# Two ready times in the plan of TensorE's work: the first tokens' key and query rows, and the sample's attention weights

## The chip, the cores and the metric

The kernel runs on one core of one Trainium2 chip. The metric is device time in microseconds (us) of one execution. The kernel before takes 1882.4 us, the median of three timed runs (1882.38 to 1887.38).

## What is computed

One step of a hybrid encoder layer, for a prompt of 2048 new tokens and a sample of 64 further tokens of a stream with 4096 past ones. The width is 1024, all data is float32. Shortened:

```python
h = rmsnorm(x, norm_g) @ w_in                      # 1024 -> 6144 columns
qa, ka, va, za, qb, kb, vb, zb, ga, gb = split(h)
qa, ka = rmsnorm(qa, qn_g), rmsnorm(ka, kn_g)      # per head and half, 64 wide
# branch A, 4 heads: two softmaxes of 64-wide halves, ALiBi, block-causal in chunks of 64
s = einsum(qa, ka) * 64 ** -0.5 - slope * |q_pos - k_pos|
p = softmax(where(allowed, s, -inf))
oa = (p[:, 0] - lam * p[:, 1]) @ va
# branch B, 4 heads: retention in chunks, with a state per head
ob = (qb @ kb.T * decay) @ vb + xi * qb @ state
oa = rmsnorm(oa, subln_g) * 0.2 * silu(za)
ob = rmsnorm(ob) * silu(zb)
y = x + (sigmoid(ga) * (oa @ w_oa) + sigmoid(gb) * (ob @ w_ob)) @ w_out
```

The prompt's tokens attend to each other, the sample's 64 tokens to the cache of 4096 keys and values and to themselves. Keys, values and retention states are outputs too.

## The kernel before

Every float32 matmul of the projections is done as three: each operand is split into a high part (a cast to fp32r, names ending in h or "hi") and a low part (the rest, l or "lo"), and high x high, high x low and low x high are added up in PSUM. ScalarE makes the high parts, VectorE or GpSimd the low ones.

**Stages.** The prompt goes through the input projection in two halves of 1024 tokens. In the first half the value, key and query columns come first, 512 columns at a time over tiles of 128 tokens (L1137 in `mm_group`). Each tile is finished by a routine of its own: `fin_va` for values, `fin_qk` for keys and queries. The other columns of the first half are done by Strassen's scheme (L989 in `strassen`). Beside these runs the sample's attention: per head nine score blocks (`sample_attn`, L2055 to L2057), their softmax, and in `sample_pv` the product with the values (L2258). When the last head is done, the x of the second half is scaled (`x_scaled`, L514 on TensorE and L528 on VectorE) and split (`x_split`, L561 and L563), to stand ready when the first half ends. The second half's projection (L1137, 256 or 288 tokens at a time for the transposed columns) then runs between blocks of the prompt's attention (scores L1880 and L1881, transposed weights L1992, product with the values L1970 to L1972) and of retention (L2337 to L2410). The last columns (L1566) and the output stage (from L2673) follow.

**Who sets the order.** Nothing is ordered by hand; the lists of TensorE, ScalarE and VectorE stand in the order in which the program was built. The kernel builds it with a planner of its own: each routine is a Python generator that issues instructions and yields the time at which it can go on. The class keeps a clock for each engine (`self.pe`, `self.act`, `self.dve`, `self.pool`, `self.dma`) and moves it by a fixed cost for each instruction. `loop` always resumes the routine of best priority whose time has come on TensorE's clock. So a number that a routine yields is not a wait on the chip: it decides behind how many other instructions the routine's next ones are put in the list. On the chip semaphores make an instruction wait for its data, and what stands behind it in the engine's list waits with it.

```python
LAT = 250.0
SLACK = 400.0
LAND = 2000.0
def P(self, cycles):
    self.pe += cycles / 2.4 + 13.0
    return self.pe + LAT
def V(self, n, ready=0.0, rate=1.05):
    self.dve = max(self.dve, ready) + rate * n + 155
    return self.dve + LAT
```

Numbers are nanoseconds of the plan. Buffers are planned in the same way: `take` waits for one, `give` states when it is free again. Buffers that the steps touch: "ev" (3), "thi" (1) and "tlo" (2) in `fin_qk`; "ath" (2), "atl" (2) and "V" (2 in the first half) in the sample's attention; the PSUM banks "mm", "s" and "at" (2 each), "pv" and "tp" (1 each).

**The two places.** In `fin_qk` the rows of a tile are multiplied by their inverse roots (L1325, VectorE, into `raw`); then four transposes (L1340) put them into bank "tp", ScalarE and VectorE take high and low parts (L1355 and L1356 for keys, L1350 and L1351 for queries), and SP's queue stores them. `t0` is the tile's first token: it is 0 for the first tile of the first half only, once for keys and once for queries. In `sample_pv` the weights of a head are transposed in five groups (L2273, into bank "at"); for each of two parts ScalarE casts (L2287), VectorE subtracts (L2289), and `mms` multiplies them with the split values (L2258). The part's ready time is what `parts` holds; `mms` yields it ahead of its matmuls. The weights themselves come from L2241, which needs rows that were swapped between partitions by way of memory (row<-swap).

## Time and profile before

| what | value |
|---|---|
| median of the timed runs | 1882.4 us |
| the profiled execution's own time | 1886.05 us |
| its span, first to last instruction | 1883.4 us |
| TensorE busy (PE) | 1866.8 us, 11090 matmuls |
| weight loads (PEld) | 1644.6 us |
| VectorE (DVE), ScalarE (ACT), GpSimd (POOL) | 1328.1, 975.3, 678.6 us |
| granted TensorE clock | 1.000 on average |

How to read it: PE is TensorE's matmuls, PEld its weight loads, which run beside them; SPq is the queue from which the DMAs are issued. A row of a timeline has the start, the duration, the engine, the line, the operation, what is written and read, and how many like ones follow each other; in brackets stands how long the engine was idle before it, and what ended that. Matmul records overlap: the time that one takes from the list is the distance from its start to the next one's. A row of waits has the total, the number of times and the longest. A row of a stage table has the stretch and its length, then the busy time of PE, PEld, DVE, ACT and POOL with the numbers of instructions, the granted clock, the DMA share and GB/s. A row for one line of the kernel has minimum, median and maximum duration in nanoseconds and the first and last start.

### The profile page before, as it was taken

To read this page: it belongs to the slowest core of one execution; us is meant where nothing else is said; L and a number is where in the kernel's file an instruction comes from. 1 tells how busy PE (TensorE), PEld (TensorE's weight loads), DVE (VectorE), ACT (ScalarE), POOL (GpSimd) and SP (SyncE) were. 2 spreads that over 40 slices of the span, in tenths; PEclk is the share of its full clock that TensorE was granted. 3 is DMA by queue.
4 is the path that set the end of the run, shared out by engine and by line. 5 is a ranking of instruction groups with operands and counts; after the bars stand their busy time and mean duration, and the time that the engine had idled before them with its cause. 6 is when DMAs were issued, how large, how long until landed. Compare 5 with 4: busy or idle time off the path is not lost.

```text
span 1883.4 us, 33013 instructions
## 1 busy us (share of the span) xinstructions
PE 1866.8 (99%) x11090; PEld 1644.6 (87%) x11090; DVE 1328.1 (71%) x3112; ACT 975.3 (52%) x2266; POOL 678.6 (36%) x728
## 2 busy tenths in 40 slices
PE   9999999999999999999999999999999999999999
PEld 7788878888888789888988889899999999998887
DVE  6765856658585678787587877777876769887664
ACT  6444545554434566555455655556666446654221
POOL 2420366555552122122210344253224555532442
PEclk9999999999999999999999999999999999999999
DMA  7654555666767967565523659446437988886552
GB/s 255 216 175 123 161 166 169 176 200 198 240 189 186 253 198 190 152 174 169 145 72 101 172 136 238 129 123 154 126 109 234 259 250 255 263 257 211 165 157 78
DMA packets 402555, 340.07 MB, mean 181 GB/s; under 512 B 85329, under 2 KB 348625, under 8 KB 401362
## 3 DMA queue, kind: packets, MB, share of 16 engines
q1 hardware_dynamic: 402386, 337.97, 61.8%
q8 instruction: 87, 1.43, 0.3%
q14 instruction: 82, 0.67, 0.1%
HBM read 218.27 MB, written 118.75 MB: 179 GB/s over the span
## 4 chain that ended last, share of the span: by engine, by line
PE 82%; DMA 7%; DVE 5%; ACT 2%; SPq 2%; issue 1%; POOL 1%; DVEq 0%; ACTq 0%; POOLq 0%
PE mm L1137 27%; PE mm L989 8%; PE tp L989 4%; PE at L1992 3%; PE s L1880 2%; PE s L1881 2%; PE s L989 2%; PE pv L1972 2%; PE pv L1971 2%; PE pv L1970 2%; DMA ws<-in_w_in_dram 2%; PE s L2799 1%; PE s L2798 1%; PE s L2797 1%; SPq L280 1%
## 5 line engine op out<-in xcount | busy, mean ns | idle before, releaser
L748 POOL TENSOR_TENSOR wl<-ws,wh 128x512 fp32r<-128x512 f32 x107 | 148.9, 1402 | 256.4 <-ACT wh L727 181.5
L1137 PE MATMUL mm<-wh,xh 128*128 128x512 f32 x504 | 203.0, 403 | 0.0
L1137 PE MATMUL mm<-wh,xl 128*128 128x512 f32 x504 | 198.2, 393 | 0.0
L1137 PE MATMUL mm<-wl,xh 128*128 128x512 f32 x504 | 198.0, 393 | 0.1
L1137 PE MATMUL mm<-xh,wh 128*128 128x288 f32 (+2 forms) x544 | 179.8, 330 | 0.0
L1137 PE MATMUL mm<-xh,wl 128*128 128x288 f32 (+2 forms) x544 | 175.6, 323 | 0.0
L1137 PE MATMUL mm<-xl,wh 128*128 128x288 f32 (+2 forms) x544 | 175.5, 323 | 0.0
L1920 ACT ACTIVATE row<-row,a_mx 128x1024 f32<-128x1024 f32 (+7 forms) x144 | 149.8, 1042 | 11.9 <-DVE a_mx L1899 11.9
L2008 DVE TENSOR_TENSOR atl<-at,ath 128x512 fp32r<-128x512 f32 (+1 forms) x144 | 92.6, 658 | 76.6 <-ACT ath L2006 76.3
L2006 ACT CAST ath<-at 128x512 fp32r<-128x512 f32 (+1 forms) x144 | 79.1, 564 | 106.6 <-PE at L1992 106.0
L856 POOL TENSOR_TENSOR wl<-ws,wh 128x256 fp32r<-128x256 f32 x64 | 54.8, 856 | 199.0 <-ACT wh L847 198.9
L1747 POOL TENSOR_TENSOR r_y<-r_y,r_sq 128x256 f32<-128x256 f32 x32 | 28.3, 884 | 238.2 <-DVE r_sq L1744 154.5
L1137 PEld LDWEIGHTS mm<-wh,xl 128*128 128x128 f32 x504 | 94.6, 188 | 21.5
L1137 PEld LDWEIGHTS mm<-wl,xh 128*128 128x128 f32 x504 | 95.0, 188 | 18.5 <-POOL wl L748 0.9
L1137 PEld LDWEIGHTS mm<-wh,xh 128*128 128x128 f32 x504 | 94.8, 188 | 17.8 <-DVE raw L1308 0.2
L1137 PEld LDWEIGHTS mm<-xh,wh 128*128 128x128 f32 x544 | 102.4, 188 | 7.2
L1137 PEld LDWEIGHTS mm<-xl,wh 128*128 128x128 f32 x544 | 102.5, 188 | 6.9
L1137 PEld LDWEIGHTS mm<-xh,wl 128*128 128x128 f32 x544 | 102.3, 188 | 6.6
L1889 DVE CUSTOM_DVE_ANT_0 row<-s,dfar 128x512 f32<-128x512 f32 (+2 forms) x141 | 87.1, 629 | 23.8 <-PE s L1881 18.0
L1942 DVE SCALAR_TENSOR_TENSOR row<-row,a_w 128x1024 f32<-128x1024 f32 (+5 forms) x88 | 96.9, 1106 | 0.0
L1880 PE MATMUL s<-K,q 128*128 128x512 f32 (+3 forms) x240 | 90.5, 378 | 1.2 <-DVE a_acc L1889 1.2
L727 ACT CAST wh<-ws 128x512 fp32r<-128x512 f32 x111 | 67.7, 620 | 41.4 <-DMA ws<-in_w_in_dram 12.7
(543 smaller groups left out, 6075.4 us busy)
## 6 DMA issues: line engine op xcount, KB each, us to landing
ws<-in_w_in_dram SPq DMA_DIRECT2D x155, 256.0 KB, 3.5
q<-qT SPq DMA_DIRECT2D x128, 128.0 KB, 3.9
K<-kT SPq DMA_DIRECT2D x48, 256.0 KB, 4.7
V<-vN SPq DMA_DIRECT2D x24, 512.0 KB, 5.9
row<-in_x_prompt_dram SPq DMA_DIRECT2D x16, 512.0 KB, 4.6
wz<-in_w_in_dram SPq DMA_DIRECT2D x32, 256.0 KB, 4.3
row<-in_cache_k_T_dram SPq DMA_DIRECT2D x32, 256.0 KB, 3.2
row<-in_cache_v_diff_dram SPq DMA_DIRECT2D x32, 256.0 KB, 3.8
```

The costliest lines, as they stand in the source:

```text
L727: self.nc.scalar.copy(h, st)
L748: eng.tensor_sub(l, st, h.bitcast(F32))
L856: nc.gpsimd.tensor_sub(l[:, cs], src, h[:, cs].bitcast(F32))
L989: nc.tensor.matmul(ps, w[:, c], xs[x][c], start=bool(tag) and c == 0 and i == 0, stop=c == 3 and i == 2, skip_group_check=True)
L1137: nc.tensor.matmul(ps, p, q, start=c == 0 and i == 0, stop=c == KC - 1 and i == 2)
L1880: nc.tensor.matmul(ps, q1s, kk, start=True, stop=False)
L1889: nc.vector.tensor_tensor_reduce(out=row[:, k0:k0 + n], in0=ps, in1=tab, scale=-SLOPES[h], scalar=3.0e38, op0=ALU.add, op1=ALU.min, accum_ ...
L1920: nc.scalar.activation(u, u, AF.Exp, bias=mx, scale=-1.0, accum_out=lp[:, k:k + 1])
L1942: nc.vector.scalar_tensor_tensor(out=u0, in0=u1, scalar=w[:, 0:1], in1=u0, op0=ALU.mult, op1=ALU.add)
L1992: nc.tensor.transpose(at[:, w:w + 128], src, self.ident)
L2006: nc.scalar.copy(ah[:, :w], at[:, :w])
L2008: nc.vector.tensor_sub(al[:, :w], at[:, :w], ah[:, :w].bitcast(F32))
```

## The change

Two ready times are raised. In `fin_qk` the first tile's transposes may come 2000 ns after the plan's end of the row, where it was 400 (for keys and for queries, tokens 0 to 127 only). In `sample_pv` every part of the weights counts as ready 2000 ns after its low part, where it was 500.

```diff
@@ fin_qk @@
             nc.vector.tensor_mul(raw3, raw3, rs.unsqueeze(2).to_broadcast([r, ng, 64]))
-            t = self.V(n + 100) + SLACK
+            t = self.V(n + 100) + (LAND if t0 == 0 else SLACK)
             yield t
@@ sample_pv @@
                 nc.vector.tensor_sub(s[:, :, 1], c, s[:, :, 0].bitcast(F32))
                 t2 = self.V(64 * nt, t2)
-                parts.append((a, tag, t2 + 500))
+                parts.append((a, tag, t2 + LAND))
             self.give("at", t2)
```

Each engine has the same number of instructions as before (10790 on TensorE, 3114 on VectorE, 2039 on ScalarE, 733 on GpSimd, 1544 DMAs on SP); a few are put into another bank. But since every later decision of the planner hangs on its clocks, the order of the lists is another one from the first edited place on: on TensorE from the 372nd instruction to the 7767th, behind which its list is the same row for row but for the names of buffers.

On TensorE at the first key tile (mm is the projection of a later tile, raw the normalised key rows of the first), this piece of the difference:

```order
 L1137 MATMUL mm<-wl,xh_120 128x512
 L1137 MATMUL mm<-wh,xl_121 128x512
+L1137 MATMUL mm<-wh,xh_120 128x512
+L1137 MATMUL mm<-wl,xh_120 128x512
+L1137 MATMUL mm<-wh,xl_121 128x512
+L1137 MATMUL mm<-wh,xh_120 128x512
+L1137 MATMUL mm<-wl,xh_120 128x512
+L1137 MATMUL mm<-wh,xl_121 128x512
 L1340 MATMUL tp<-ident,raw 128x128 x4
 L1137 MATMUL mm<-wh,xh_120 128x512
```

Six matmuls of the projection have moved ahead of the four transposes; the transposes stand at place 378 in place of 372.

On TensorE at the first head's product with the values (at is the bank of the transposed weights, atp a split part of them, vhl the split values; L989 is Strassen's scheme), before:

```order
L2273 MATMUL at<-ident,row 128x128 x8
L989 MATMUL mm<-S1h,wh 128x512
L989 MATMUL mm<-S1l,wh 128x512
L989 MATMUL mm<-S1h,wl 128x512
L989 MATMUL mm<-S1h,wh 128x512
L989 MATMUL mm<-S1l,wh 128x512
L989 MATMUL mm<-S1h,wl 128x512
L989 MATMUL mm<-S1h,wh 128x512
L989 MATMUL mm<-S1l,wh 128x512
L989 MATMUL mm<-S1h,wl 128x512
L2258 MATMUL pv<-vhl,atp 128x256 x8
```

The same eight matmuls in the order of the change, with the eleven rows that end in the next transposes:

```order
L989 MATMUL tp<-xh_122,wh 128x512
L989 MATMUL tp<-xl_123,wh 128x512
L989 MATMUL tp<-xh_122,wl 128x512
L2055 MATMUL s<-ath,qq 128x512
L2056 MATMUL s<-atl,qq 128x512
L2057 MATMUL s<-ath,qq 128x512
L989 MATMUL tp<-xh_122,wh 128x512
L989 MATMUL tp<-xl_123,wh 128x512
L989 MATMUL tp<-xh_122,wl 128x512
L2258 MATMUL pv<-vhl,atp 128x256 x8
L2273 MATMUL at<-ident,row 128x128 x4
```

The eight rows of transposes that stood together are now two groups of four (places 1282 and 1301), and a score block of the next head and more of Strassen's scheme stand ahead of the matmuls, which move from place 1260 to 1320. Over the four heads the lag grows: the last L2258 stands at 2486 in place of 2402, the first L514 of the second half's x at 2509 in place of 2425, and the first half's last L989 at 2665 in both. The first score of the prompt's attention (L1880) stands at 2858 in place of 2801.

On TensorE in the second half, where retention blocks run between projection and attention (row is their working memory, tp and pv the banks that they choose from; L2410 transposes one block's result, L2371 and L2374 make the next block's), before, with buffer numbers:

```order
L2410 MATMUL tp_7565<-ident_106,row_6182 128x128 x4
L1880 MATMUL s_7571<-K_6616,q_7099 128x512
L1881 MATMUL s_7571<-K_6616,q_7099 128x512
L1137 MATMUL mm_7487<-xh0_120,wh_7401 128x512
L1137 MATMUL mm_7487<-xl0_121,wh_7401 128x512
L1137 MATMUL mm_7487<-xh0_120,wl_7402 128x512
L2371 MATMUL tp_7588<-row_6182 128x128
L2374 MATMUL tp_7588<-row_6182 128x128
```

In the order of the change, of another block of the same half:

```order
L1137 MATMUL mm_8873<-wh_8865,xh0_120 128x512
L1137 MATMUL mm_8873<-wl_8866,xh0_120 128x512
L1137 MATMUL mm_8873<-wh_8865,xl0_121 128x512
L2410 MATMUL tp_8922<-ident_106,row_6259 128x128 x4
L2371 MATMUL tp_8946<-row_6259 128x128
L2374 MATMUL tp_8946<-row_6259 128x128
```

Both use the single bank "tp"; nothing stands between them here, which the order before has at no block.

## Prediction

> **What bounds the kernel now.** I read the page first: the span, the share of each engine, and the granted clock in 40 slices.
>
> ```profile
> span 1883.4 us, 33013 instructions
> PE 1866.8 (99%) x11090; PEld 1644.6 (87%) x11090; DVE 1328.1 (71%) x3112; ACT 975.3 (52%) x2266; POOL 678.6 (36%) x728
> PEclk9999999999999999999999999999999999999999
> ```
>
> TensorE (PE) is busy in 1866.8 of 1883.4 us at full clock, so 16.6 us is all that a better order could win. The second view is busy time by stage. The columns that matter are the first two: length of the stage, and PE's busy time in it.
>
> ```profile
> 0.00:75.00 75.00, 73.42 (x352) 58.89 (x353) 46.08 (x106) 47.22 (x96) 29.17 (x31) 1.00 0.79 260
> 75.00:300.00 225.00, 222.68 (x1019) 179.45 (x1018) 150.77 (x340) 104.67 (x262) 71.15 (x80) 1.00 0.53 155
> 300.00:560.00 260.00, 259.18 (x1210) 212.08 (x1209) 172.03 (x373) 122.73 (x326) 145.74 (x181) 1.00 0.66 199
> 560.00:660.00 100.00, 95.54 (x548) 83.61 (x547) 60.75 (x166) 49.76 (x117) 21.79 (x19) 1.00 0.81 214
> 660.00:1450.00 790.00, 788.74 (x5119) 716.27 (x5118) 582.87 (x1626) 466.85 (x1059) 223.66 (x283) 1.00 0.55 152
> ```
>
> PE is idle for 1.6 us in the opening, 2.3 us in the first projections and the sample's first head, 0.8 us in the rest of the first half, 4.5 us where attention begins, and only 1.3 us in the 790 us after that. The third view, PE's waits, names what ended them (total, times, longest):
>
> ```profile
> PE pv L1970 <- ACT ath L2006: 1.6, 1, 1.6
> PE tp L1880 <- DMA q<-qT: 1.4, 1, 1.4
> PE s L1880 <- DVE a_acc L1889: 1.2, 1, 1.2
> PE tp L1340 <- DVE raw L1325: 1.1, 1, 1.1
> PE pv L2258 <- DVE atp L2289: 0.9, 1, 0.9
> ```
>
> The last two rows are the places that the change edits: transposes (L1340) of the first key tile, which wait for the normalised row (L1325), and matmuls (L2258) with the sample's weights, which wait for their low part (L2289). The two are 2.0 of the 2.3 us of their stage. PE works its list in order, so each matmul behind them waits too.
>
> **The change, part by part.** It adds no instruction and no semaphore: the counts of each engine are equal in the two orders. Only ready times of the plan move, and the plan's order follows.
>
> First part, the first key tile:
>
> ```profile
> 82.77 0.40 PE L1137 MATMUL mm<-wl,xh 128*128 128x512 f32 x1
> 83.01 0.40 PE L1137 MATMUL mm<-wh,xl 128*128 128x512 f32 x1
> 84.50 0.66 PE L1340 MATMUL tp<-ident,raw 128*128 128x128 f32 x4 [1.09 <-DVE raw L1325]
> 83.75 0.69 DVE L1325 TENSOR_TENSOR raw<-raw,sm_y 128x512 f32<-128x512 f32 x1
> ```
>
> Matmuls of 512 columns start 0.24 us apart (82.77 to 83.01), and 0.23 us apart in longer runs: records overlap, so the pace is the start-to-start time, not the 0.40 us of one. Without a wait the transposes would have started at 83.01 + 0.23 = 83.24; they started at 84.50, a loss of 1.26 us (1.09 shown as idle, the rest hidden under the record before). In the new order six more matmuls stand ahead of them: 6 x 0.23 = 1.39 us. That is longer than 1.26, so the wait goes, by 0.13 us of margin. Nothing on VectorE that makes the row is moved ahead of that point (the row is its 128th instruction in both orders). Term: **-1.3 us**; if VectorE were late by more, the part beyond 0.13 us stays, so between -1.3 and 0. The cast behind the transposes (L1355, ScalarE), the low part (L1356, VectorE) and the two stores of the tile on SP's queue come some 0.1 us later than they did, as the transposes do. The second edit of this part, the query tile, had no idle PE in the list; I cost it at nothing, covered by the projection matmuls that stand around it.
>
> Second part, the sample's weights:
>
> ```profile
> 280.32 0.40 PE L989 MATMUL mm<-S1h,wl 128*128 128x512 f32 x1
> 281.64 1.60 PE L2258 MATMUL pv<-vhl,atp 128*128 128x256 f32 x8 [0.92 <-DVE atp L2289]
> 278.77 1.82 DVE L2241 SCALAR_TENSOR_TENSOR row<-row,s_den 128x1024 f32<-128x1024 f32 x1 [1.94 <-DMA row<-swap]
> 289.77 1.14 PE L2258 MATMUL pv<-vhl,atp 128*128 128x256 f32 x8
> ```
>
> Without a wait the eight would have started at 280.32 + 0.23 = 280.55: 1.09 us lost; and they took 1.60 us where the next eight took 1.14, another 0.46 us. The cause is upstream: a load (row<-swap) held VectorE for 1.94 us, and the weights' low part came behind it. In the old order 13 instructions stood between the four transposes (L2273) that feed the first four of the eight and the matmuls; in the new order 34 do, some 5 us more, so I take the 1.55 us as gone. Term: **-1.5 us**, between -1.5 and 0.
>
> What is late next is the strand of the sample itself. Its last matmul moves from the 2402nd to the 2486th place, 84 x 0.23 = 19.4 us later. No PE time is lost by that alone: Strassen matmuls (L989) of the same half take the places ahead, and the half ends at the 2665th place in both orders. The buffers that the strand holds longer (two each of the split tiles, two of the values, one accumulator bank) make only ScalarE, VectorE and SP wait, none of which is full.
>
> Third, what the shifted plan does elsewhere. Orders differ from the 372nd PE instruction to the 7767th; the output stage behind is the same on PE. I looked for banks of PSUM that are refilled sooner than they can be emptied and found one new place: a retention block's four transposes (L2410) are followed directly by another block's matmuls (L2371) into the same bank, which occurs nowhere in the old order. The price is in rows of a block before:
>
> ```profile
> 700.93 0.60 PE L2410 MATMUL tp<-ident,row 128*128 128x128 f32 x4
> 701.57 0.59 ACT L2413 COPY row<-tp 128x512 f32<-128x512 f32 x1 [2.38 <-PE tp L2410]
> 702.53 0.38 PE L2371 MATMUL tp<-row 128*128 128x128 f32 x2
> ```
>
> The four issue in about 0.4 us (to 701.37), and ScalarE's copy, which must empty the bank, ends at 702.16. There a score block and projections filled the time; at the new place nothing does, and PE waits 0.8 us and a semaphore's way, if ScalarE is free. Term: **+0.9 us**, between 0.8 and 1.9 (one softmax piece of about 1 us ahead of the copy).
>
> The rest of the reorder I cost at nothing, with bounds: below, the idle time from 300 to 1450 us all goes (0.8 + 4.5 + 1.3 = 6.6 us); above, the long stretch gets as much as the stage where attention begins has, 4.5 us, and that stage keeps its own. Nothing is nearest, since the 790 us stretch shows 1.3 us after a like plan.
>
> Sum: -1.3 - 1.5 + 0.9 = **-1.9 us**. The profiled execution took 1886.05 us, 2.65 us around its span; by the sum it would take 1884.1. The median of the three timed runs is 1882.4, 3.65 us under the profiled one, so I forecast 1882.4 - 1.9 = **1880.5 us**.
>
> **The rivals.**
>
> *The gain is given back in the hand-over to the second half.* Rows of the second half's x are scaled (L528) once the sample is done and then split (L563) on VectorE:
>
> ```profile
> L528 DVE SCALAR_TENSOR_TENSOR row<-row,gT,rb x24: 472/953/1058, 544.7 to 566.2; 128x256 f32<-128x256 f32 x24
> L528 DVE SCALAR_TENSOR_TENSOR xT<-xT,gT,rb x8: 471/714/960, 536.5 to 542.4; 128x256 f32<-128x256 f32 x8
> L563 DVE TENSOR_TENSOR xl<-xT,xh x4: 680/689/1445, 580.7 to 583.6; 128x512 fp32r<-128x512 f32 x4
> 587.64 0.28 PE L1137 MATMUL mm<-xh,wh 128*128 128x256 f32 x1
> ```
>
> Scaling ran from 536.5 to about 567.0, 30.5 us for 32 pieces, and the first split was ready at 584.3 for a first matmul at 587.64. Now scaling starts 19.4 us later, at 555.9. The new order puts 29 of its pieces ahead of the last of the first four splits: 29/32 of 30.5 is 27.6, so 583.5, and with four splits of 0.69 us about 586.3, 1.3 us ahead of need. If all 32 had to come first, 586.4 plus the 3.6 us that the four took gives 590.0, 2.4 us late: 1882.9. For it: pieces of 0.95 us where the fast ones took 0.47. Against: VectorE was idle for about 10 us between 567 and 585, where the late pieces now fall:
>
> ```profile
> DVE u L1002 <- issue: 4.9, 1, 4.9
> DVE xl L563 <- ACT xh L561: 3.4, 2, 3.2
> DVE u L1002 <- PE tp L989: 2.0, 1, 2.0
> ```
>
> With small waits like it elsewhere the time is 1881.5 to 1884.
>
> *Slower: a query load behind a blocked store.* SP's queue is in order, and the attention blocks' loads share it with stores that wait for engines:
>
> ```profile
> SPq L285 <- DVE r_o L1750: 51.0, 13, 10.8
> q<-qT SPq DMA_DIRECT2D x128, 128.0 KB, 3.9
> 617.69 0.36 PE L1880 MATMUL tp<-K,q 128*128 128x256 f32 x1 [1.40 <-DMA q<-qT]
> ```
>
> A store held the queue for up to 10.8 us; a load of queries lands 3.9 us after its issue. Where the shifted plan puts such a store ahead of a block's load, PE waits at the block's first score (L1880). It decides when the hold exceeds the time the plan left over the 3.9 us; the one case before cost 1.4 us, the worst hold would cost 10.8 - 3.9 = 6.9 us, so 1880.5 + 6.9 = 1887.4 us, or 1882 for the small case. Against: 128 loads, and only three short waits for them, all at the start of attention. In this trace the granted clock is full in all slices and no idle row of PE is over 1.6 us. [...]
>
> *Faster than forecast.* The 4.5 us where attention begins is planned anew: its first scores (L1880) come 57 instructions later, at the pace of the projection there,
>
> ```profile
> 595.79 0.28 PE L1137 MATMUL mm<-xh,wl 128*128 128x256 f32 x1
> 595.91 0.28 PE L1137 MATMUL mm<-xh,wh 128*128 128x256 f32 x1
> ```
>
> 57 x 0.12 = 6.8 us, while the splits that release their loads end perhaps 4 us later. If all of it goes: 1880.5 - 4.5 = 1876.0.
>
> *The change doesn't do what it says.* If both edited waits stay (VectorE late at the first; the load row<-swap later still at the second), only the +0.9 is left: 1883.3.
>
> **How the numbers follow.** Chances: the forecast (1879 to 1881.5) 0.43; given back 0.22; both waits stay 0.05; slower by the queue or another wait of its size, 1885 to 1892, 0.18; faster 0.12. The likeliest is 1880.5. The range runs from 1875.5 (the faster case and a little of the opening) to 1888.0 (the worst hold), leaving out about 0.14 above and 0.05 below. About 0.3%, 5.6 us, is what a measurement of this kernel can tell from no change: faster means under 1876.8, slower over 1888.0. From the cases: faster 0.11, within 0.3% 0.75, slower 0.14.
>
> **What would show it.** Right: no idle row at the first L1340 and the first L2258; a wait of about 0.9 us at one L2371 with the releaser L2413; PE's busy time unchanged near 1866.8; the 790 us stretch again with one or two us idle. Wrong: PE idle over 5 us in the hand-over, a wait for q<-qT of several us, or a wait for rows of a kind that the list of before doesn't have. A time outside 1875.5 to 1888 would mean that the reorder, which I cost at nothing, weighs more than the two edits.

## The result: 0.24% slower

| | median of the executions | lowest to highest | executions |
|---|---|---|---|
| before | 1883.25 us | 1880.71 to 1887.38 | 20 |
| the change | 1888.61 us | 1886.22 to 1891.62 | 20 |

The ratio is 1.0024, with an interval of 1.0018 to 1.0029. The change costs about 4.5 us (0.0024 x 1883), 5.4 us by the two medians. The forecast was 1880.5 us, and the range ended at 1888.0, 0.6 us under the median. By the bound of 0.3% the two kernels are the same, but the intervals leave no doubt of the sign.

### The profile page after: what moved, and what is told of

Read it like the earlier page. It is cut to its first block, busy times and chain, and to the rows that moved or that the text cites. A ratio compares the mean times of both kernels' runs of the same rounds, so it can differ in the third digit from the quotient of the medians.

```text
span 1885.1 us, 32987 instructions
## 1 busy us (share of the span) xinstructions
PE 1868.8 (99%) x11090; PEld 1647.8 (87%) x11090; DVE 1329.7 (71%) x3112; ACT 976.0 (52%) x2266; POOL 670.6 (36%) x728
## 4 chain that ended last, share of the span: by engine, by line
PE 90%; DVE 4%; DMA 3%; ACT 1%; issue 1%; SPq 0%; POOL 0%; DVEq 0%; ACTq 0%; POOLq 0%
PE mm L1137 30%; PE mm L989 9%; PE tp L989 5%; PE at L1992 3%; PE s L1881 2%; PE s L1880 2%; PE s L989 2%; PE pv L1972 2%; PE pv L1971 2%; PE pv L1970 2%; PE mm L1566 1%; PE s L2797 1%; PE s L2799 1%; PE s L2798 1%; DMA ws<-wsum 1%
## 5 line engine op out<-in xcount | busy, mean ns | idle before, releaser
L748 POOL TENSOR_TENSOR wl<-ws,wh 128x512 fp32r<-128x512 f32 x107 | 145.7, 1372 | 233.6 <-ACT wh L727 206.7
L1137 PEld LDWEIGHTS mm<-xl,wh 128*128 128x128 f32 x544 | 102.5, 188 | 6.5
L1880 PE MATMUL s<-K,q 128*128 128x512 f32 (+3 forms) x238 | 90.2, 381 | 0.7 <-DVE a_acc L1889 0.7
L727 ACT CAST wh<-ws 128x512 fp32r<-128x512 f32 x111 | 67.5, 619 | 44.3 <-DMA ws<-in_w_in_dram 16.2
```

What stands on the lines that cost most here:

```text
L727: self.nc.scalar.copy(h, st)
L748: eng.tensor_sub(l, st, h.bitcast(F32))
L1137: nc.tensor.matmul(ps, p, q, start=c == 0 and i == 0, stop=c == KC - 1 and i == 2)
L1880: nc.tensor.matmul(ps, q1s, kk, start=True, stop=False)
```

## The profile after

The page of the changed kernel, the same three lines:

```profile
span 1885.1 us, 32987 instructions
PE 1868.8 (99%) x11090; PEld 1647.8 (87%) x11090; DVE 1329.7 (71%) x3112; ACT 976.0 (52%) x2266; POOL 670.6 (36%) x728
PEclk9999999999999999999999999999999999999999
```

The span is only 1.7 us longer than the one shown of before. Here two profiles mislead: the profiled execution of before was a long one (its span of 1883.4 us stands against a median span of 1881.4 over 29 executions), and that of the change a short one (1885.1 against 1886.3 over 20). Medians give 4.9 us, and a place that loses it has to be looked for in several traces.

Busy time by stage, first the changed kernel, then before for the stretch behind 1450 us, which the prediction did not quote. The boundaries of the last two rows are the same rows of TensorE's list in both: 1426.26 and 1428.21 is the row behind the 7767th, from which on the two lists are equal (the first of the last 780 L1566; "row 7767" below), then come the first L2673 and the first L2797.

```profile
75.00:300.00 225.00, 223.05 (x1016) 180.56 (x1015) 149.99 (x343) 103.13 (x260) 70.47 (x79) 1.00 0.52 153
300.00:560.00 260.00, 259.31 (x1222) 212.95 (x1221) 161.46 (x358) 124.88 (x331) 144.51 (x184) 1.00 0.65 200
560.00:660.00 100.00, 96.76 (x548) 84.61 (x547) 62.85 (x166) 46.59 (x104) 19.79 (x17) 0.98 0.78 211
660.00:1450.00 790.00, 788.09 (x5124) 716.39 (x5123) 597.25 (x1640) 470.63 (x1071) 222.43 (x285) 1.00 0.56 154
1426.26:1526.31 100.05, 98.99 (x784) 98.37 (x783) 72.02 (x115) 48.59 (x94) 54.19 (x38) 1.00 0.86 248
1526.31:1717.91 191.60, 189.58 (x1538) 188.33 (x1537) 148.71 (x274) 109.08 (x279) 78.29 (x67) 0.99 0.81 243
```

```profile
1428.21:1526.47 98.26, 98.26 (x785) 98.26 (x784) 74.10 (x118) 49.59 (x95) 53.41 (x37) 1.00 0.85 244
1526.47:1716.60 190.13, 187.81 (x1539) 186.75 (x1537) 151.66 (x273) 109.38 (x279) 80.29 (x68) 1.00 0.82 246
```

The hand-over (560 to 660 us), where the prediction feared a loss, has 3.2 us idle in place of 4.5; the 790 us stretch has 1.9 in place of 1.3. What is worse lies behind row 7767, where TensorE's list did not change: the last columns (L1566) take 100.05 us in place of 98.26, in which TensorE had not been idle at all, and the first part of the output stage 191.60 in place of 190.13.

PE's waits in the changed kernel (total, times, longest):

```profile
PE at L2674 <- DVE ogl L2630: 1.9, 3, 1.6
PE mm L1137 <- ACT wh L727: 1.7, 1, 1.7
PE mm L1137 <- DVE raw L1308: 1.2, 1, 1.2
PE pv L2410 <- DVE row L2404: 0.9, 1, 0.9
PE mm L1137 <- POOL wl L748: 0.9, 1, 0.9
PE s L1566 <- DVE ev L1586: 0.8, 1, 0.8
PE mm L1137 <- ACT raw L1305: 0.7, 1, 0.7
PE tp L2371 <- ACT row L2413: 0.7, 1, 0.7
```

Both edited waits are off the list, and the predicted stall of L2371 is there with 0.7 us. New are the waits for raw L1308 and raw L1305, for weights at the hand-over (L727, L748), for row L2404, and for an eviction (an instruction of VectorE that empties a bank of PSUM) at L1566. The first key tile shows where the wait for L1308 comes from (timeline):

```profile
79.03 3.51 DVE L881 TENSOR_TENSOR row<-xh,xl 128x512 f32<-128x512 f32 x2
83.05 0.69 DVE L1325 TENSOR_TENSOR raw<-raw,sm_y 128x512 f32<-128x512 f32 x1
83.66 0.68 DVE L1308 TENSOR_TENSOR raw<-mm,gk 128x512 f32<-128x512 f32 x1
84.40 0.50 PE L1137 MATMUL mm<-wh,xh 128*128 128x512 f32 x1 [1.23 <-DVE raw L1308]
85.89 0.60 PE L1340 MATMUL tp<-ident,raw 128*128 128x128 f32 x4
```

The transposes no longer wait, as forecast. But the projection matmul that has moved ahead of them needs a bank "mm" that VectorE's L1308 empties, and on VectorE L1308 stands right behind L1325, which makes the transposed rows. In the order before this second need was covered by the first wait: L1308 began at 84.36 and the matmul at 85.10. With the first wait gone, the second costs 1.2 us in its place. At the query tile, where nothing waited before, the same happens: the matmul behind the four transposes (143.49) waits 0.7 us for ScalarE's L1305 to empty its bank "mm".

## The experiments

Three theories stood at the start. By the first, the loss comes from what the two ready times do directly, and grows with the delay that they add. By the second, one of the two parts does it. By the third, it comes from the order of the second half, which the planner writes anew on all engines, whatever the delay. The later runs ask which instruction of that order costs the time.

All runs in one table. The columns are distances between the same rows of TensorE in each trace, in us: the first half (span's start to the last L989), the middle (to row 7767), the last columns (to the first L2673) and the output stage (to the end of the last matmul). "half" counts the stretches of about 3.4 us at half clock in the last two (about 1.7 us lost in each, an estimate from half of its length, contained in the column). The order of the second half is before's (b) or the change's (c): from about the 2500th matmul on, the lists of every kernel tried are one of these two but for what an experiment edits.

| kernel | order | first half | middle | last columns | output | half | ratio to before, interval |
|---|---|---|---|---|---|---|---|
| before | b | 587.4 | 840.8 | 98.3 | 353.1 | 0 | 1 |
| e0_before | b | 586.2 | 840.2 | 98.3 | 354.7 | 1 | 0.9999 (0.9990 to 1.0008) |
| e4_sample_1500 | b | 584.5 | 840.7 | 98.7 | 353.0 | 0 | 0.9994 (0.9985 to 1.0003) |
| e5_both_3000 | b | 585.8 | 840.1 | 98.3 | 351.9 | 0 | 0.9998 (0.9990 to 1.0007) |
| the change | c | 585.1 | 841.2 | 100.1 | 354.9 | 1 | 1.0024 (1.0018 to 1.0029) |
| e1_keyquery | c | 586.5 | 842.9 | 100.8 | 356.9 | 1 | 1.0036 (1.0022 to 1.0050) |
| e2_sample_2000 | c | 587.0 | 840.2 | 100.8 | 354.0 | 0 | 1.0029 (1.0018 to 1.0040) |
| e3_ws_first | c | 585.1 | 841.7 | 99.7 | 355.5 | 0 | 1.0015 (1.0006 to 1.0023) |
| e13_spread_only | c | 585.5 | 840.1 | 101.4 | 355.5 | 1 | 1.0024 (1.0013 to 1.0034) |
| e6_xl_behind | c | 585.1 | 840.1 | 109.0 | 353.6 | 3 | 1.0054 (1.0041 to 1.0066) |
| e8_xl_wst | c | 584.8 | 841.5 | 109.8 | 349.9 | 3 | 1.0035 (1.0023 to 1.0048) |
| e7_wst_pool | c | 585.6 | 841.8 | 102.2 | 351.6 | 1 | 1.0007 (0.9998 to 1.0016) |
| e10_xl_wst | c | 586.5 | 840.8 | 101.1 | 352.0 | 0 | 1.0005 (0.9996 to 1.0014) |
| e11_all | c | 586.7 | 839.6 | 102.5 | 350.0 | 1 | 1.0002 (0.9993 to 1.0012) |
| e12_all_spread | c | 585.7 | 841.9 | 101.6 | 351.3 | 0 | 1.0004 (0.9993 to 1.0015) |
| e14_ws_pool | c | 586.0 | 840.7 | 105.1 | 351.2 | 1 | 1.0021 (1.0012 to 1.0030) |
| e15_ws_wst_pool | c | 585.9 | 840.4 | 100.2 | 350.1 | 0 | 1.0001 (0.9992 to 1.0010) |

The half-clock stretches are in the last columns in e6, e7, e8, e11 and e14, else in the output stage. In e6 and e8 three of them stand in a row (10.24 us). The middle has one more in every trace but those of before, e2, e6, e10, e11, e13 and e15.

### The parts and the size of the delay

The kernel before once more, as a yardstick (no edit).

> The kernel before, unchanged, as a yardstick with spans and granted clocks for every run. Two theories are asked of it. Order theory: the loss of 5 us came with another order of the second half, and 3.4 us of it are two falls of TensorE's clock to half, 1.7 us each; then the runs of this kernel show a clock of 1.000 or 0.999 (no fall, or one), a span near 1880.5 where the clock is 1.000, and the ratio is 1.000 within 0.0005. Clock theory as rival: the falls strike every order alike; then the clocks here scatter from 0.997 to 1.000 as they did with the change, and the falls explain none of the difference.

1884.09 us, ratio 0.9999. Its last columns are again 98.3 us. Its executions have clocks from 0.999 to 1.000, but the one in the profile 0.998, with two half-clock stretches (one in the middle): the falls strike this order too, which is the rival's point.

One part alone, the key and query tile (edit: the second hunk of the diff is left out):

```diff
-                parts.append((a, tag, t2 + LAND))
+                parts.append((a, tag, t2 + 500))
```

> The first edit alone: the first tile's key and query rows count as ready 2000 ns later, the sample's weights as before (500 ns). The first half keeps the sample's places of before, but from TensorE's matmul 2463 on every engine's list is that of the whole change. Theory of the late lists: the loss lies behind matmul 7767, where TensorE's list is equal in all kernels but VectorE's, ScalarE's, GpSimd's and SP's are not; then this kernel takes 1887 to 1890 us, ratio 1.002 to 1.0035, with 14 to 15 us for the 100 matmuls of L1566 that run in 12.6 us in the kernel before, and over 40 us for the second hundred of L2673. Sample theory as rival: the sample's move costs the time; then it takes 1882 to 1884 us.

1889.98 us, ratio 1.0036. The other part alone, the sample's weights (edit: the first hunk is left out):

```diff
-            t = self.V(n + 100) + (LAND if t0 == 0 else SLACK)
+            t = self.V(n + 100) + SLACK
```

> The second edit alone: the sample's weights count as ready 2000 ns later, the first tile's rows as before. In the lists of all engines the rows behind the sample's third head (TensorE from matmul 1628 on) are those of the whole change, the second half with them. Order theory: the time is that of the whole change less the 1.5 us that the first tile's wait costs there too, so between 1886 and 1889 us, ratio 1.002 to 1.003, with the same waits between 615 and 625 us (for wh of L727, 1.9 us, and for wl of L748, 1.2 us) and a clock below 1.000. Key theory as rival: the six matmuls moved at the first key tile and what follows from them cost the time; then this kernel takes 1881 to 1883 us.

1889.69 us, ratio 1.0029. Each part alone costs as much as both: the loss is no sum of two parts, and the theory of the parts falls.

The sample's part alone with a smaller delay, and both parts with a larger one:

```diff
-                parts.append((a, tag, t2 + LAND))
+                parts.append((a, tag, t2 + 1500))      # e4; first hunk left out
+                parts.append((a, tag, t2 + 3000))      # e5; first hunk kept
```

> The second edit alone and smaller: 1500 ns in place of 500, not 2000. The first half is reordered much as in the change (the sample's matmuls move back as well), but from TensorE's matmul 2503 on every engine's list is that of the kernel before. Order theory: the sample's waits (L2258 on L2289) go, the second half is as before: 1880.5 to 1883 us, ratio 0.9990 to 1.0000, no new wait at 615 to 625 us. Delay theory as rival: the sample's later end holds up the scaling of the second half's x, and the loss grows with the delay; then two thirds of it are here, 1885 to 1887 us, with TensorE idle between 580 and 625 us.

> Both edits, the second one larger still: first tile 2000 ns as in the change, sample 3000 ns. From TensorE's matmul 2503 on every engine's list is that of the kernel before. Order theory: 1880.5 to 1883.5 us, ratio 0.9990 to 1.0003, although both edits are in, with the wait of the first key tile still there in its new place (L1137 on L1308, 1.2 us). Delay theory: the sample ends later than in the change, so the loss is at least that of the change, 1888 us or more.

1882.85 us (0.9994) and 1883.44 us (0.9998). A delay of 3000 ns for the sample costs nothing where 2000 costs 4.5 us, so the theory of the delay falls too. What goes with the time is the order column: the four traces with order b spend 98.3 to 98.7 us in the last columns, the five with order c that leave the output stage's queue as it is and compute the same (the change, e1, e2, e3, e13) 99.7 to 101.4; with 1.7 us taken off for a half-clock stretch, the output stage has 351.9 to 353.1 against 353.1 to 355.5. The means are 98.4 and 100.6 us for the last columns, 352.8 and 354.3 for the output stage: 2.2 and 1.6, together 3.8 us, from one trace of each kernel. In the middle the two orders overlap, also with these stretches taken off (838.4 to 840.8 against 839.5 to 841.2); the means there are 839.2 and 840.2, so up to 1 us more may be lost in it. The theory of the order stands. e4 and e5 also give the worth of the edits themselves, free of the other order: -0.5 us and +0.1 us by the medians, both within the noise.

### Where the hand-over waits

At the start of the middle the changed kernel waits for weights whose load (ws) stood on SP's queue behind four stores:

```profile
611.72 3.82 SPq L285 DMA_DIRECT2D qbT<-ev  x4
615.64 0.37 SPq L280 DMA_DIRECT2D ws<-in_w_in_dram  x1
619.81 0.50 PE L1137 MATMUL mm<-wh,xh 128*128 128x512 f32 x1 [1.66 <-ACT wh L727]
```

The edit issues two of these loads ahead of the stores:

```diff
-            self.wst.append((st, self.ld(st, src, 1 << 18), shape))
+            self.wst.append((st, self.ld_first(st, src, 1 << 18), shape))
...
+    def ld_first(self, dst, src, nbytes=0):
+        held, self.held = self.held, []     # stores of qbT, kept back until here
+        t = self.ld(dst, src, nbytes)
+        self.held = held
+        self.let_go()
+        return t
```

> The change with two weight loads (ws) of the hand-over put ahead of the qbT stores that stood in front of them in SP's queue; the lists of all other engines are those of the change, SP's differs in 14 rows. Theory of the late lists: the load goes out some 4 us earlier than 615.6 us, ScalarE's L727 no longer waits 3.1 us for it, and the waits of L1137 for wh (1.9 us) and wl (1.2 us) go or shrink; but this stage had not lost against the kernel before (840 to 843 us from the end of the first half to matmul 7767 in either order), so the gain of 1 to 4 us comes on top of it and the loss behind matmul 7767 stays: 1885 to 1888 us. Hand-over theory as rival: the whole loss is here, 1882 to 1884 us.

1887.89 us, ratio 1.0015. The wait fell from 1.66 to 0.95 us, but the interval (1.0006 to 1.0023) overlaps that of the change (1.0018 to 1.0029): by the ratios 1.7 us are won (0.0009 x 1883), which these runs can't tell from nothing. The loss against before stays, and with it 99.7 us in the last columns and 355.5 in the output stage.

### The output stage: one load on SP's queue

In the changed kernel, rows of SP's queue, GpSimd, ScalarE and TensorE in the output stage:

```profile
1562.02 0.36 SPq L285 DMA_DIRECT2D mT<-mo  x1
1564.08 1.33 POOL L2613 TENSOR_TENSOR on<-on,z 128x528 f32<-128x528 f32 x1 [2.70 <-DMA on<-obT]
1566.95 1.77 POOL L2539 TENSOR_TENSOR wt43l<-wst,wt43h 128x512 fp32r<-128x512 f32 x1
1568.75 0.55 SPq L280 DMA_DIRECT2D wst<-in_w_out_dram  x1
1570.51 0.46 SPq L280 DMA_DIRECT2D ga<-gaT  x1
1574.07 0.92 ACT L2641 ACTIVATE ga<-ga,bg 128x264 f32<-128x264 f32 x2 [5.42 <-DMA ga<-gaT]
1581.38 0.39 PE L2674 MATMUL at<-ogl,w_o_reth 128*128 128x264 f32 x1 [1.55 <-DVE ogl L2630]
```

SP's queue issues nothing from 1562.38 to 1568.75, 6.4 us: its next entry refills a buffer (wst) that GpSimd still reads in L2539 until 1568.72, and GpSimd is itself late by 2.70 us for a load. Behind that entry stand the gates (ga), for which ScalarE is idle for 5.42 us; its casts for L2630 come behind, and TensorE waits for L2630. In e0_before the same ScalarE row waited 2.52 us for its ga. The edit issues this one load, the seventh of w_out, from GpSimd's own queue, where it stands behind L2539 anyway:

```diff
-                    t = self.ld(st[k], self.i["w_out"][0, 512 * k + 128 * ct:512 * k + 128 * ct + 128]
+                    t = self.ld_pool(st[k], self.i["w_out"][0, 512 * k + 128 * ct:512 * k + 128 * ct + 128]
...
+    self.nc.gpsimd.dma_start(dst, src)      # load no. 7 only
```

> The change with one DMA moved: the load of output weights that held SP's queue from 1562 to 1568.7 us, because GpSimd still read its buffer, is issued from GpSimd's own queue, where it stands behind that reader. TensorE's, VectorE's and ScalarE's lists are those of the change. Theory of the late lists: the gate loads (ga<-gaT) behind it are issued some 6 us earlier, ScalarE's L2641 no longer waits 5.4 us, the high and low parts of og (L2627, L2630) come in time, and the second hundred of L2673 takes 36 to 38 us in place of 40.5: 3 to 4 us less than the change, 1884.5 to 1886 us. Hand-over theory as rival: it stays at 1888 to 1890 us. Should GpSimd's issue of the load delay its own work (L2613), the gain is smaller.

1885.25 us, ratio 1.0007. The rows of e7:

```profile
1567.14 0.46 SPq L280 DMA_DIRECT2D ga<-gaT  x1
1571.55 0.87 POOL L3149 DMA_DIRECT2D wst<-in_w_out_dram  x1 [0.30 <-POOL wt43l L2539]
1571.71 0.92 ACT L2641 ACTIVATE ga<-ga,bg 128x264 f32<-128x264 f32 x2
```

The gates are loaded 4.4 us ahead of the refill, and ScalarE no longer waits. The output stage falls to 351.6 us, and in all seven kernels with this edit (e7, e8, e10, e11, e12, e14, e15) it lies between 349.9 and 352.0 (mean 350.9), where order c without it has 353.1 to 355.5 (mean 354.3, half-clock stretches taken off). One load's place in a queue is worth 3.5 us: more than the 1.6 us that order c loses in this stage, and nearly all of the 3.8.

That it is more than the loss has a reason that the traces show. Order b has holds of this kind too: from the first L2673 on, SP's queue waits for GpSimd's readers of these buffers (L2532 and L2539) 20.3 us in all in before and 21.4 in e0_before, 23.7 in the change and 16.5 in e7. The same edit in order b was not tried. So the runs show what the load's place is worth in order c, not that this hold alone makes the loss.

### The last columns: what was not settled

Rows of the changed kernel, then of e0_before, at the eviction of bank "s" (L1586) and the low parts of the next x (L1530):

```profile
1485.36 0.65 ACT L1527 CAST xh<-xraw 128x544 fp32r<-128x544 f32 x1 [5.04 <-DMA xraw<-xd]
1486.04 0.72 DVE L1530 TENSOR_TENSOR xl<-xraw,xh 128x544 fp32r<-128x544 f32 x1 [4.13 <-ACT xh L1527]
1488.72 0.41 DVE L1586 TENSOR_TENSOR ev<-s,u 128x256 f32<-128x256 f32 x1
1489.28 0.36 PE L1566 MATMUL s<-xh,wh 128*128 128x256 f32 x1 [0.76 <-DVE ev L1586]
```

```profile
1482.41 0.41 DVE L1586 TENSOR_TENSOR ev<-s,u 128x256 f32<-128x256 f32 x1
1483.11 0.45 DVE L1586 TENSOR_TENSOR ev<-s,u 128x288 f32<-128x288 f32 x1
1486.58 0.72 DVE L1530 TENSOR_TENSOR xl<-xraw,xh 128x544 fp32r<-128x544 f32 x1 [3.02 <-ACT xh L1527]
```

In both kernels VectorE idles for a load of x. In order b the evictions of the bank stand ahead of the waiting L1530, in order c behind it, so the bank comes free 6.3 us later (1488.72 for 1482.41; row 7767 stood at 1426.26 and 1426.36), and TensorE waits. The theory was that moving L1530 behind the evictions takes the 2 us back.

```diff
-                self.nc.vector.tensor_sub(l[:, c:c + 544], self.xraw[:, c:c + 544], h[:, c:c + 544].bitcast(F32))
+                self.xl_late(s, l[:, c:c + 544], self.xraw[:, c:c + 544], h[:, c:c + 544].bitcast(F32))
...
+    self.xlate.append([args, AFTEREV, s])   # pieces 17 to 20: emitted behind AFTEREV more L1586
```

> The change with one thing undone on VectorE: the four low parts of one pass of x (L1530), each put behind the next four evictions of L1586, as the kernel before has them; TensorE's, ScalarE's and GpSimd's lists are those of the change, SP's differs in a few places around it. Theory of the late lists: the evictions that free bank s no longer stand behind an L1530 that waits for its load until 1485.4 us, the wait of L1566 for L1586 goes, the hundred matmuls take 12.6 us in place of 14.4 to 15.2: 1.8 to 2.6 us less than the change, 1886 to 1887 us. Hand-over theory as rival: what costs the time is the wait for weights at 615 to 625 us; then it stays at 1888 to 1890 us.

> Both of these edits in the change. Theory of the late lists: the two losses are separate and add, 5 to 6.5 us less than the change: 1882 to 1884 us, ratio to the kernel before 0.9995 to 1.0003, although the hand-over with its waits at 615 to 625 us is untouched. Hand-over theory as rival: 1888 to 1890 us still, or the time reappears as another wait within the output stage.

1893.02 us (1.0054), and with the load of e7 as well 1889.37 (1.0035): slower. In these two kernels a held low part is taken from an x that the next load has already overwritten, so one low part belongs to the x of another pass, and VectorE has to wait for that load; TensorE waited for it 8.5 us in e6, and the clock fell to half meanwhile. They say nothing of the theory. They do say once more what the load on GpSimd's queue is worth: 1893.02 - 1889.37 = 3.65 us.

The same with fewer L1586 between (4, 4, 2 and 0), so that no load comes between, and with the load of e7; e11 has the edit of e3 besides:

```diff
+LATEXL, AFTEREV = (16, 17, 18, 19), (4, 4, 2, 0)
```

> The change with both late lists mended: the output weight load from GpSimd's queue, as in the run before it, and of the low parts of x (L1530) of that one pass the first three put behind the evictions of bank s, but all four still ahead of the load that overwrites their source. Theory of the late lists: the hundred matmuls of L1566 take 12.6 to 13 us in place of 14.4 to 15.2, the second hundred of L2673 36 to 38 us in place of 40.5; 1882 to 1884 us, and at least 1 us less than with the load moved alone (1885.3). Rival: L1566 then waits at the next bank (at) for the evictions that the three low parts push back, and nothing is gained over 1885.3 us.

> All three edits of the last runs in the change: weight loads first at the hand-over, output weight load from GpSimd's queue, low parts of x behind the evictions. Theory of the late lists: the gains add: 1879 to 1882 us, under the kernel before (1883) as well, ratio 0.998 to 0.9995. Rival: every wait taken away comes back at the next one, and the time stays at 1883 us or above.

1885.73 us (1.0005) and 1885.04 (1.0002). The last columns are not shorter: 101.1, and 102.5 - 1.7 = 100.8 us. PE's waits in that stretch, of e10:

```profile
PE at L1566 <- DVE ev L1586: 2.1, 1, 2.1
```

The wait has moved from bank "s" to bank "at", whose evictions now stand behind the low parts. Spreading the low parts out further (four L1586 behind each, the next load of x held back with them), together with all other edits and alone:

```diff
+    self.xlate.append([(dst, src), self.xlate[-1][1], self.xlate[-1][2]])   # the load of xraw
+LATEXL, AFTEREV = (16, 17, 18, 19), 4
```

> The kernel with all three edits, but the four low parts of x (L1530) of that pass spread out: each behind four more evictions of L1586 than in the change, one between two evictions, and the next load of raw x behind the last of them, which is the kernel before's order. TensorE's, ScalarE's and GpSimd's lists stay. Theory of the late lists: in the run with all three edits the wait had only moved from bank s to bank at (2.4 us at L1566, and a fall of the clock behind it); spread out it goes, the hundred matmuls take 12.6 us, and the time is 2 to 4 us less than with the three edits: ratio to the kernel before 0.998 to 0.9995. Rival: the evictions are late for another reason (GpSimd's work beside VectorE's, the load of raw x itself), and the wait stays above 1.5 us at one bank or the other, ratio 1.000 or above.

> The change with only this one thing undone, the low parts of x spread behind the evictions; the output weight load and the hand-over as the change has them. Theory of the late lists: 1.8 to 2.6 us less than the change, the waits of L1566 for L1586 gone, the waits of L2674 for L2630 and 40 us for the second hundred of L2673 still there; ratio to the kernel before 1.001 to 1.002. Rival: TensorE arrives earlier at L2674 and waits there for the same late ScalarE instead, so that nothing is gained: ratio 1.0024 or more.

1884.71 us (1.0004) and 1889.42 us (1.0024). Now the wait is at bank "mm" (2.3 and 2.2 us), and the last columns stay at 101.6 and 101.4. Alone, the edit changes nothing of the loss. So VectorE's order at this one place is not the cause, or not the only one.

The traces show a second place, one pass of x later. Rows of e13_spread_only (L3149 is L1530 there), then of e0_before:

```profile
1503.90 0.73 DVE L3149 TENSOR_TENSOR xl<-xraw,xh 128x544 fp32r<-128x544 f32 x1 [5.93 <-ACT xh L1527]
1504.54 0.42 DVE L1586 TENSOR_TENSOR ev<-mm,u 128x256 f32<-128x256 f32 x1
1505.11 0.36 PE L1566 MATMUL mm<-xh,wh 128*128 128x256 f32 x1 [2.17 <-DVE ev L1586]
```

```profile
1500.72 0.42 DVE L1586 TENSOR_TENSOR ev<-mm,u 128x256 f32<-128x256 f32 x1 [3.54 <-PE s L1566]
1502.61 1.62 DVE L1530 TENSOR_TENSOR xl<-xraw,xh 128x544 fp32r<-128x544 f32 x1
```

In order b the evictions of bank "mm" stand ahead of the next pass's first low part, in order c behind it, and the edits move the low parts of one pass only. In the change that low part does not wait (1502.55); in e12 to e14, where the load of that x goes out later (in e13 at 1494.39, in the change at 1492.58), it waits for more than 5 us, and TensorE behind it. No run mended both passes, so the theory of the late lists is neither shown nor refuted for the last columns.

A second candidate is SP's queue. The evictions write buffers (ev) which stores on it must empty. In e13 the first of them ends at 1482.00 and its store (gaT) goes out at 1489.26, in e0_before at 1482.82 and 1484.63: loads of ws whose buffers GpSimd's L748 has yet to free stand ahead of it. (In the change the eviction itself ends only at 1489.13, and the store goes out at 1490.09.) So the last two runs issue three of the ws loads from GpSimd's queue, e14 on top of e12, e15 with the load of e7 and VectorE's order left as the change has it (lines of e15):

```diff
-            self.wst.append((st, self.ld(st, src, 1 << 18), shape))
+            self.wst.append((st, self.ld_ws(st, src, 1 << 18), shape))
...
+    self.nc.gpsimd.dma_start(dst, src)      # ws loads no. 104, 105 and 106
```

> The kernel with all edits of the run before it (weight loads first at the hand-over, output weight load from GpSimd's queue, low parts of x spread), and three further weight loads (ws<-wsum) of the last columns issued from GpSimd's queue, whose own L748 frees their buffers. In SP's queue these loads stood ahead of the gaT stores and waited up to 3 us for L748. Queue theory: VectorE's evictions (L1586, ev) waited for those stores to free their buffer; the stores go out 3 to 4 us earlier, the wait of 2.3 us at L1566 goes, the hundred matmuls around it take 12.6 us, and the time falls by 2 to 3 us: ratio to the kernel before 0.9985 to 0.9997. Rival: the wait comes from VectorE's own list or from GpSimd's work beside it, or the weights land later from GpSimd's queue; it stays above 1.5 us, ratio 1.000 or above.

> The change with four loads in GpSimd's queue: the output weight load and the three weight loads (ws<-wsum); the hand-over and VectorE's list are those of the change. Queue theory: SP's queue alone makes the loss behind matmul 7767, so the wait of 2.2 us at L1566 shrinks to what VectorE's low parts of x cost (0 to 1 us): 1 to 2 us less than with the output weight load alone, ratio to the kernel before 0.9995 to 1.0003. List theory as rival: VectorE's list (L1530 ahead of the evictions of bank s) is enough for the wait: ratio 1.0005 to 1.0012, as with the output weight load alone.

1887.86 us (1.0021) and 1884.58 us (1.0001). e14 is worse. ScalarE waits 5.24 us for one of the weights that GpSimd now loads, and SP's queue waits 7.8 us for L748, with the stores (gbT) and the load of the next x behind it. VectorE then waits 5.74 us for a store, and 5.28 us at the next pass's low part, behind which the eviction of bank "mm" stands: TensorE waits 4.58 us for it.

e15 has no loss left against before, but it doesn't win it where it was lost: its last columns take 100.2 us, like the change's, with two waits for evictions (0.9 and 0.6 us), and its output stage 350.1, some 3 us less than before's 353.1. Against e7 (1.0007, 0.9998 to 1.0016) its 1.0001 (0.9992 to 1.0010) is no difference that these runs can tell.

So the cause of the 2 us in the last columns stays open. That they are there in every trace of order c is shown; that waits for evictions carry them is read from the traces (1.1 of the 1.8 us in the change's own); which instruction of the order makes them was tried four times on VectorE, at one of two passes, and twice on the queue, and none of it brought the 98.3 us back. No version came out below before by more than its interval.

## Why the prediction was wrong

**The first key tile (-1.3 us).** The wait at the transposes went, but the term came out with the other sign. The next instruction in VectorE's list, L1308, holds a bank that the matmuls moved ahead need: TensorE waits for it 0.8 to 2.2 us (mean 1.3) in the thirteen traces with this edit. The wait that went was 0.2, 0.2, 1.1 and 1.3 us in the four traces without it; the 1.26 us of the prediction were one execution's. The prediction said that nothing of VectorE's work that makes the row moves; it did not ask what else the six matmuls wait for. Before, one wait stood for two. And the query tile, costed at nothing, has a new wait of 0.7 us for L1305 in all thirteen and in none of the four: 2.0 us of waiting at the two tiles, by these means, where there had been 0.7.

**The sample's weights (-1.5 us).** The wait is gone, as forecast. With order b, where it can be seen alone, the whole time moved by -0.5 us (e4), with an interval from -2.8 to +0.6 us (0.9985 and 1.0003 of 1883). The size of 1.5 us is neither confirmed nor excluded.

**The stall of L2371 behind L2410 (+0.9 us).** Right: 0.7 us, with the releaser and the bank that were named. A second new stall of retention was not found: L2410 waits for VectorE's L2404, 0.8 to 1.1 us, in the traces of order c and in none of order b.

**The rest of the reorder, costed at nothing.** This is the step that failed, and in it the words "the output stage behind is the same on PE". They are true, and they are why the place was not looked at. But behind TensorE's row 7767 the lists of the other engines go on differing: VectorE's to its 2954th row of 3114, ScalarE's to the 1897th of 2039, GpSimd's to the 683rd of 733, and SP's to the 1401st DMA of 1544. TensorE does the same work there and waits for other engines at other times: 3.8 us by the traces (2.2 in the last columns, 1.6 in the output stage), of the 4.5 that the whole change costs by the ratio. The upper bound of 4.5 us was taken from the waits where attention begins; that it is near the loss is luck, since it was given to the middle, which lost 1 us at the most, and counted as a tail.

**The rival "a query load behind a blocked store".** The mechanism was right, the place wrong. SP's queue was held by an entry that waited for an engine, and a load behind it came late: not a store ahead of queries, but a refill (wst) ahead of gates (ga), held for 6.4 us. The prediction had priced 10.8 us of hold at 6.9 us of loss; taking these 6.4 us away won some 3.5, with ScalarE and VectorE between the load and TensorE. The median lies in the band of 1885 to 1892 us that it had been given, with a chance of 0.18. The waits for queries went: among PE's waits of 0.4 us and more in the changed kernel none is for q<-qT.

**The rival "given back in the hand-over".** It did not come as priced. From 560 to 660 us TensorE did 548 matmuls in both kernels, although in the change it waited for weights there (1.7 and 0.9 us) and 3.4 us ran at half clock; the waits for queries had gone.

**What was not thought of** is that the two edits only tip the planner into one of two second halves. For the sample's weights 1500 and 3000 ns give b, 2000 gives c, and the key and query edit alone gives c as well. Among these kernels the size of the delay says nothing of the time.

## What to carry to other kernels

Where a planner writes the order, compare the lists of all engines and of the DMA queue, not only that of the engine that bounds the kernel: an equal list on TensorE is no equal time. When a wait is to be hidden, look at what the instructions put in its place wait for; if it is made by the same engine a row later, only the label of the wait changes. And before a small loss is put down to a number that was edited, try the number smaller and larger: if the loss comes and goes, it belongs to the order that came out, and an edit at the place which loses (here one load on another queue) is worth more than the edited number.

## What the runs showed of the hardware

**Stretches at half clock.** The granted clock fell to half (0.50) for about 3.4 us at two places of the changed kernel, though no idle row of TensorE there is longer than 1.7 us. The stage table around them (length, PE's busy time first, the clock third from the end):

```profile
617.35:620.76 3.41, 1.30 (x5) 0.52 (x3) 1.13 (x5) 1.62 (x4) 0.93 (x1) 1.00 0.77 233
620.76:624.17 3.41, 3.00 (x9) 2.42 (x10) 1.08 (x4) 2.47 (x7) 0.35 (x1) 0.50 0.84 260
1579.90:1583.30 3.40, 1.77 (x12) 1.56 (x13) 3.40 (x6) 2.89 (x8) 2.01 (x2) 1.00 1.07 348
1583.30:1586.70 3.40, 3.40 (x18) 3.40 (x18) 3.37 (x6) 1.71 (x5) 3.38 (x3) 0.50 0.53 180
```

In the 3.4 us ahead of each, TensorE was busy for 1.30 us (38%) and 1.77 us (52%). In e13_spread_only a stretch of 3.41 us with 1.66 us (49%) was followed by no fall, and one with 1.30 us (38%) was:

```profile
1501.28:1504.69 3.41, 1.66 (x13) 1.42 (x11) 0.79 (x2) 1.19 (x2) 0.00 (x0) 1.00 0.42 101
1579.79:1583.20 3.41, 1.30 (x9) 0.89 (x8) 3.41 (x6) 2.99 (x8) 2.10 (x2) 1.00 1.01 281
1583.20:1586.60 3.40, 3.40 (x17) 3.40 (x17) 3.40 (x6) 2.81 (x7) 2.48 (x2) 0.51 0.97 296
```

A stretch that was 52% busy thus came ahead of a fall and one that was 49% busy did not: the busy share of a stretch alone does not tell whether a fall follows, and what decides it was not shown. The same kernel runs with and without them: the profile of before has no such stretch, the one of e0_before has two. Both orders have them, so they don't make the difference, but they may widen it: the mean granted clock was 0.9983 over the 20 executions of the change and 0.9991 to 0.9995 over those of before in the several sets of runs, 0.0008 to 0.0012 of 1885, so an estimate of 1.5 to 2.3 us at the most.

**VectorE beside GpSimd.** In the changed kernel, with the first L881 already shown:

```profile
78.99 3.00 POOL L1103 TENSOR_TENSOR wl<-ws,wh 128x512 fp32r<-128x512 f32 x2 [6.36 <-ACT wh L1093]
89.19 1.28 DVE L881 TENSOR_TENSOR row<-xh,xl 128x512 f32<-128x512 f32 x2
```

Two adds of 128x512 (L881) took 3.51 us at 79.03, beside two subtractions of GpSimd, and 1.28 us at 89.19, where GpSimd was idle. These 2.2 us stand ahead of L1325, the normalised rows of the first tile, in both kernels (3.50 us in before).
